# Reordering the helper work at the two ends of a Strassen-tiled ConvFFN: low parts, SiLU, the transfers of E and the last roundings

## The chip, the core and the metric

The kernel runs on one core of one Trainium2 chip. The metric is the device time of one execution in microseconds (us). A core has a matrix engine (TensorE, PE in the rows, its weight loads PEld), VectorE (DVE), ScalarE (ACT), GpSimd (POOL) and SyncE (SP, which here only issues DMAs). Each engine runs its own instructions in program order, and waits where an operand or a buffer isn't ready.

## The reference

A trunk of two residual layers on x of 1024 rows and 1024 columns, all float32. Layer 0 has a gated DeltaNet and a ConvFFN; then K and V are projected once; layer 1 has a chunked attention and a ConvFFN; a final RMSNorm ends it. The change touches the ConvFFN alone, which both layers have:

```python
def conv_ffn(xn, w_up, conv_w, conv_b, w_down):
    h = causal_dwconv(xn @ w_up, conv_w) + conv_b          # w_up 1024 x 5632, 3 taps
    gate, val = h[..., :FFN_DIM], h[..., FFN_DIM:]          # FFN_DIM = 2816
    return (jax.nn.silu(gate) * val) @ w_down

for layer in range(DEPTH):
    ...
    h = h + conv_ffn(rmsnorm(h, f_norm[layer]), f_w_up[layer], f_conv[layer], f_conv_b[layer], f_w_down[layer])
return rmsnorm(h, final_norm)
```

## The kernel before

**Numbers.** A float32 operand is cut into a high part (`uh`, `xh`: the value rounded to fp32r, a CAST on ScalarE) and a low part (`ul`, `xl`: value less high part, a TENSOR_TENSOR on VectorE or GpSimd). Each product is three matmuls: high by high (L1391), low data by high weight (L1392), high data by low weight (L1393).

**Tiles.** The up-projection has 22 channel tiles j of 128 gate and 128 value channels. Tiles 1 to 21 are each computed by seven products n = 1 to 7 in the manner of Strassen. `left_sum(j, n)` forms the weight sum of product n in place on VectorE (`r21`, `r11`, `r12` are the raw weight blocks, `r` in the rows), `operand(j, n)` rounds it on ScalarE (`uh`) and takes the low part (`ul`). The data sums `h<-h,h` with their roundings (`x7`, `xt2`, `xt1`, `xt4`, high and low) are made once at the start of the FFN. `after(j, n)` reads the accumulator banks: a copy `keep` on ScalarE for n = 1, `keep` and `keep7` on VectorE for n = 6, `vpre` and `gpre` for the rest. Product 2 adds onto the bank of product 1, and 4 onto that of 7, so each has to wait for the copy of that bank (`keep`, `keep7`).

**After a tile** come the three convolution taps of the value (`val`, v0 to v2) and of the gate (`gate`, g0 to g2): the first tap on ScalarE (ACTIVATE, L1483), the other two on VectorE (L1486). Then `silu` on ScalarE (L1489; with a table load where the table in the engine is another), `gated` (value times gate, VectorE), and `hidden` for the last three tiles (`hidh` on ScalarE, `hidl` on VectorE).

**The down-projection** runs in nine groups `("d", g, n)`, mixed into the same sequence; its weights are `a`, its roundings `dh`, `dl` and, for the channels, `eh`, `el`. Results go through `stage` tiles to DRAM by DMAs that add (`send`, issued by GpSimd). The product E is held apart in `d_e`: in the last group `load_e(u)` reads it back and `send_e(u, n)` adds it to three totals (n = 6, 7, 4) by three DMAs of 512 KB on GpSimd. The last weights of the down-projection, `fr`, are loaded by `load_last` and rounded by `cut_last(q)`: `fh` on ScalarE, `fl` on VectorE for even q and on GpSimd for odd q.

**What sets the order.** TensorE's work is a list of steps of 12 matmuls each: 0 to 7 are plain, 8 to 22 are the products of tiles 1 and 2 and the first of tile 3, 23 to 217 products of the tiles 3 to 21 with the down-projection's steps between them; the last up-projection steps are 211 (21,1), 212 (21,7), 213 (21,6), 214 (21,5), 215 (21,2), 216 (21,4) and 217 (21,3). Everything on the other engines is a job, placed by `at(i, f, rank)` in front of step i; jobs of one step are issued in the order of rank, and an engine keeps that order. `operand(j, n)` is placed two steps ahead of its product with rank 1. For the steps 8 to 16 (`i < early`) its low part is a job of its own on VectorE; later it is GpSimd's. `sums`, `highs` and `lows` of the data have ranks 1 to 2. The ring of up-projection weight parts has three buffers, those of `d` and `e` two. Weight loads of the up-projection are issued by SyncE (L1437).

```python
if i < early:
    low = []
    at(i - 2, lambda j=j, n=n, low=low: low.append(operand(j, n, False)), 1)
    at(i - 2, lambda low=low: low[0](), 2.5)
...
at(i + 2 + k // 2, lambda u=u, n=n: send_e(u, n), 0.6)
at(last_at[q], lambda q=q: cut_last(q), 1.5)
```

`fin_at` is the index of the last down-projection step of the last group, `pos[j, s]` the step at which tile j's part s starts, `nx(j, s)` that of tile j + 1, `end` the start of the last part.

Of the kernel before, what the change touches and what calls it, by code (L numbers as in the profile page):

```python
# [22 lines left out]
FP = 22  # L23
# [5 lines left out]
def trunk_kernel(  # L29
# [1323 lines left out]
    def ffn(layer, h, hp, xs, tail, d_r, last):  # L1353
# [19 lines left out]
        def at(i, f, rank=1):  # L1373

            jobs.setdefault(max(i, 0), []).append((rank, f))

        def cut_high(src, ring, copy=nc.scalar.copy):
            hi, lo = [(wd if ring == "e" else wf).tile([P, HALF], F32R, name=ring + x, tag=ring + x, bufs=RINGS[ring]) for x in "hl"]
            copy(hi, src)  # L1379
            return hi, lo  # L1380

        def cut_low(src, hi, lo, eng):
            tt(eng, lo, src, hi.bitcast(F32), sub)
# [58 lines left out]
        def left_sum(j, n):  # L1442
            a = lambda q: raw[j, q]
            if (j, n) in summed:
                return
            summed.add((j, n))
            if n == 7:
                tt(nc.vector, a(21), a(11), a(21), sub)
            elif n == 6:
                tt(nc.vector, a(21), a(22), a(21), sub)  # L1450
            elif n == 5:
                tt(nc.vector, a(11), a(21), a(11), add)
            elif n == 3:
                tt(nc.vector, a(12), a(12), a(21), sub)

        def operand(j, n, lo=True):

            a = lambda q: raw[j, q]
            left_sum(j, n)
            src = a({1: 11, 2: 12, 7: 21, 6: 21, 5: 11, 4: 22, 3: 12}[n])  # L1460
            ops[j, n] = cut_high(src, "u")
            if lo:
                cut_low(src, *ops[j, n], nc.gpsimd)
            return lambda: cut_low(src, *ops[j, n], nc.vector)
# [51 lines left out]
        def after(j, n):  # L1516
            p_ = bank[j, {2: 1, 4: 7, 3: 5}.get(n, n)]
            if n == 1:
                keep[j] = tp.tile([P, HALF], F32, name="keep", tag="keep", bufs=2)
                nc.scalar.copy(keep[j], p_)  # L1520
            elif n == 6:
                tt(nc.vector, keep[j], p_, keep[j], add)
                keep[j, 7] = tp.tile([P, HALF], F32, name="keep7", tag="keep7")
                tt(nc.vector, keep[j, 7], bank[j, 7], keep[j], add)
            elif n == 5:
                tt(nc.vector, new_pre(j, 1)[:, HALF:SEQ], p_, keep[j, 7], add)
            elif n == 2:
                nc.scalar.copy(new_pre(j, 0)[:, 0:HALF], p_)
            elif n == 4:
                tt(nc.vector, new_pre(j, 1)[:, 0:HALF], p_, keep[j], add)  # L1530
            elif n == 3:
                tt(nc.vector, new_pre(j, 0)[:, HALF:SEQ], p_, keep[j], add)
# [44 lines left out]
        end, fin_at = pos[FP - 1, 7], pos["d", NG - 1, 4]  # L1577
        early = pos["p", 1, 3]
        for i, (j, n) in due.items():
            if i < early:  # L1580
                low = []
                at(i - 2, lambda j=j, n=n, low=low: low.append(operand(j, n, False)), 1)
                at(i - 2, lambda low=low: low[0](), 2.5)
            else:
                at(i - 2, lambda j=j, n=n: operand(j, n), 1)
                if j > 3 and n in (6, 4):
                    at(i - 2, lambda j=j, n=n: left_sum(j, n - 1), 1.05)
            if n != 2 or j > 2:
                at(i + 1, lambda j=j, n=n: after(j, n), 0)

        def nx(j, s):
            return pos[j + 1, s] if j + 1 < FP else end + s
# [23 lines left out]
        for j in range(3, FP - 1):  # L1616
# [2 lines left out]

        v0, v1, v2, g0, g1, g2 = [(v, i) for v in (1, 0) for i in range(3)]  # L1620
        when = {
            0: [(11, (g0,), 0), (12, (v0,), 0), (13, (v1,), 2), (13, (v2,), 2.7), (15, (g1, g2, silu), 2), (17, (gated,), 2)],
            1: [(18, (v0, v1), 2), (19, (v2, g0), 2), (20, (g1,), 2), (21, (g2, silu), 2), (22, (gated,), 2)],
            2: [(24, (v0, v1), 2), (25, (v2, g0), 2), (26, (g1,), 2), (27, (g2, silu), 2), (28, (gated,), 2)],
        }
        for j in range(3, FP - 1):
            when[j] = [(pos[j, 7], (v0, v1), 2), (nx(j, 1), (v2, g0), 2), (nx(j, 2), (g1,), 2)]
            when[j] += [(nx(j, 3), (g2,), 2), (nx(j, 4), (silu,), 1.6), (nx(j, 5), (gated,), 2)]
            if j >= 2 * NG:
                when[j].append(({18: fin_at + 5, 19: fin_at + 7}.get(j, nx(j, 6)), (hidden,), 1.9))  # L1630
        for j, w_ in when.items():
            for i, fs, r in w_:
                at(i, lambda j=j, fs=fs: [taps(j, *f) if isinstance(f, tuple) else f(j) for f in fs], r)
# [82 lines left out]
        def total(n, u):  # L1716
            if n == 1:
                return d_e[u]
            c, s = where[n]
            return d_c[c, s, u]  # L1720
# [8 lines left out]
        def load_e(u):  # L1729
            stage["e", u] = hp.tile([P, SEQ], F32, name="stage", tag=f"h{layer + 1}_{(3, 4)[u]}")  # L1730
            nc.sync.dma_start(out=stage["e", u], in_=d_e[u])

        def send_e(u, n):
            nc.gpsimd.dma_start(out=total(n, u), in_=stage["e", u], accum_op=add)
# [21 lines left out]
        for u, i in ((0, pos["d", NG - 1, 5]), (1, fin_at + 2)):  # L1756
            at(i, lambda u=u: load_e(u), 3)
            for k, n in enumerate((6, 7, 4)):
                at(i + 2 + k // 2, lambda u=u, n=n: send_e(u, n), 0.6)


        k0 = 2 * NG
# [3 lines left out]
        last_at = [pos[FP - 1, s] for s in (3, 4, 5, 6)] + [end + 1] * 4  # L1766
        if layer == 1:
            last_at = [pos[FP - 1, 2]] + last_at[:-1]
# [16 lines left out]
        def cut_last(q):  # L1785
            k, s = slots[q]
            hi, lo = [actp.tile([P, HALF], F32R, name=f"f{x}{q}", tag=f"x{x}{k}_{s}") for x in "hl"]
            nc.scalar.copy(hi, fw[q])
            cut_low(fw[q], hi, lo, nc.gpsimd if q % 2 else nc.vector)
            fw[q] = hi, lo  # L1790

        for q in range(8):
            s = (1, 1, 2, 3, 4, 4, 5, 6)[q]
            at(fin_at + 1 if q < 2 else pos[FP - 1, s], lambda q=q: load_last(q), 1)
            at(last_at[q], lambda q=q: cut_last(q), 1.5)

        if layer == 0:

# [140 lines left out]
    d_h = [dram.tile([P, SEQ], F32, name=f"d_h{k}") for k in range(KT)]  # L1939
    xb = ([[None, None] for _ in range(KT)], [[None, None] for _ in range(KT)])  # L1940
    ctx_f, tail0 = ffn(0, h, hp, normed, tails[0], d_r0, xb)
    ctx_o = ctx.enter_context(ExitStack())
    wp = ctx_o.enter_context(tc.tile_pool(name="wp1", bufs=2, **SB))
# [288 lines left out]
    def norm_out(t, ht, fin):  # L2232
# [26 lines left out]
        return go()  # L2259

    ctx_f, _ = ffn(1, h, hp, normed, tails[0], d_r1, norm_out)
    ctx_f.close()
    ctx_h.close()
# [56 lines left out]
```

## Time and profile before

| | |
|---|---|
| median of 3 runs | 2615.96 us (2615.45 to 2617.17) |
| profiled execution | 2616.91 us, of which span 2615.1 us |
| granted clock of TensorE, mean | 0.994 |
| TensorE busy | 2517.5 us, 96% of the span |
| VectorE busy | 1862.1 us, 71% |
| ScalarE busy | 1413.1 us, 54% |
| GpSimd busy | 1485.5 us, 57% |
| up-projection and first down-projection steps of FFN0, FFN1 | 678 to 1298 us, 1932 to 2557 us |

A step of 12 matmuls takes 2.72 us where nothing is waited for. In the rows, an idle time in brackets stands in front of the instruction and names the instruction that ended it, as the profile infers it. "pu" is an accumulator bank of the up-projection, "r" a raw weight block, "x4" a group of four instructions on end.

### The profile page before, as it was taken

How to read it: one execution, taken by the hardware profiler on the slowest of the kernel's cores; microseconds unless marked ns; L12 is line 12 of the kernel's file. 1: busy time of each engine (PE TensorE's matmuls, PEld its weight loads, DVE VectorE, ACT ScalarE, POOL GpSimd, SP SyncE). 2: the span in 40 equal slices, each digit the busy share in tenths (PEclk: the TensorE clock that was granted, in tenths of full speed). 3: DMA queues.
4: the chain of work that ended last, by engine and by line, in shares of the span. 5: the costliest groups of instructions: out<-in, count | busy, mean ns of one | idle time of the engine just before them, and what ended most of it. 6: DMA issues, size and time to landing. Idle time of an engine off the chain costs nothing.

```text
span 2615.1 us, 39396 instructions
## 1 busy us (share of the span) xinstructions
PE 2517.5 (96%) x13933; PEld 2071.1 (79%) x13933; DVE 1862.1 (71%) x3102; ACT 1413.1 (54%) x2714; POOL 1485.5 (57%) x1472
## 2 busy tenths in 40 slices
PE   7999899999999999999999999998989999999998
PEld 5878788888777888888778888887867788888877
DVE  5765865554688888888775666665478788888875
ACT  5444455464455555655455555555345655555643
POOL 3655543345447777777645444443343777777771
PEclk9999999999999999999999999999999999999999
DMA  4534435555337677768831111114232567677795
GB/s 127 138 99 123 123 106 155 159 162 161 93 85 152 144 155 154 145 141 163 200 112 51 44 58 44 48 42 139 75 123 68 142 137 151 143 157 154 152 197 174
DMA packets 317590, 326.72 MB, mean 125 GB/s; under 512 B 32976, under 2 KB 240592, under 8 KB 317392
## 3 DMA queue, kind: packets, MB, share of 16 engines
q1 hardware_dynamic: 285936, 219.07, 28.5%
q0 software_dynamic: 26560, 96.48, 20.7%
q10 hardware_dynamic: 4896, 8.65, 0.9%
q8 instruction: 110, 1.80, 0.3%
q14 instruction: 88, 0.72, 0.1%
HBM read 180.94 MB, written 143.20 MB: 124 GB/s over the span
## 4 chain that ended last, share of the span: by engine, by line
PE 53%; POOL 5%; DVE 5%; issue 3%; ACT 2%; DMA 2%; DVEq 0%; POOLq 0%; ACTq 0%; SPq 0%
PE pu L1393 8%; PE pu L1391 8%; PE pu L1392 8%; PE pd L1392 4%; PE pd L1393 4%; PE pd L1391 4%; PE acc L120 3%; PE acc L121 3%; PE acc L122 3%; POOL ul L1358 2%; PE ptp L2070 2%; PE poT L2100 1%; PE poT L2099 1%; PE acco L120 1%; PE acco L121 1%
## 5 line engine op out<-in xcount | busy, mean ns | idle before, releaser
L1358 POOL TENSOR_TENSOR ul<-r,uh 128x512 fp32r<-128x512 f32 x282 | 445.7, 1600 | 297.6 <-ACT uh L1379 276.2
L120 PE MATMUL acc<-xh,whi 128*128 128x512 f32 x896 | 374.1, 418 | 0.3 <-ACT xh L1097 0.2
L121 PE MATMUL acc<-xl,whi 128*128 128x512 f32 x896 | 353.0, 394 | 1.8 <-POOL xl L379 0.9
L122 PE MATMUL acc<-xh,wlo 128*128 128x512 f32 x896 | 352.0, 393 | 0.5 <-POOL wlo L105 0.5
L105 POOL TENSOR_TENSOR wlo<-wraw,whi 128x256 fp32r<-128x256 f32 (+1 forms) x293 | 235.9, 834 | 197.7 <-ACT whi L103 157.3
L1379 ACT CAST uh<-r 128x512 fp32r<-128x512 f32 x296 | 181.9, 623 | 223.9 <-DVE r L1358 170.1
L1393 PE MATMUL pu<-xh,ul 128*128 128x512 f32 x552 | 216.6, 392 | 5.6 <-POOL ul L1358 5.5
L1391 PE MATMUL pu<-xh,uh 128*128 128x512 f32 x552 | 216.6, 392 | 3.0 <-ACT uh L1379 1.6
L1392 PE MATMUL pu<-xl,uh 128*128 128x512 f32 x552 | 215.8, 391 | 1.0 <-POOL xl L379 1.0
L1712 ACT COPY stage<-pd 128x1024 f32<-128x1024 f32 x180 | 174.9, 1013 | 50.0 <-PE pd L1393 49.4
L122 PEld LDWEIGHTS acc<-xh,wlo 128*128 128x128 f32 x896 | 168.4, 188 | 37.9 <-POOL wlo L105 0.9
L121 PEld LDWEIGHTS acc<-xl,whi 128*128 128x128 f32 x896 | 169.6, 189 | 26.6 <-POOL xl L379 3.1
L120 PEld LDWEIGHTS acc<-xh,whi 128*128 128x128 f32 x896 | 169.3, 189 | 22.9 <-ACT xh L1097 1.2
L1486 DVE SCALAR_TENSOR_TENSOR val<-vpre,colt,val 128x1023 f32<-128x1023 f32 (+2 forms) x92 | 153.4, 1668 | 38.6 <-ACT val L1483 38.4
L1358 POOL TENSOR_TENSOR dl<-a,dh 128x512 fp32r<-128x512 f32 x90 | 155.0, 1722 | 38.4 <-ACT dh L1379 38.4
L1486 DVE SCALAR_TENSOR_TENSOR gate<-gpre,colt,gate 128x1023 f32<-128x1023 f32 (+2 forms) x92 | 175.4, 1906 | 0.8
L2050 POOL TENSOR_SCALAR sS<-sS,st 128x640 f32<-128x640 f32 (+4 forms) x128 | 88.3, 693 | 140.5 <-DVE st L2049 122.7
L1358 DVE TENSOR_TENSOR r<-r,r 128x512 f32<-128x512 f32 x168 | 131.5, 782 | 31.0 <-POOL ul L1358 29.6
L2048 ACT ACTIVATE sS<-sS,st 128x640 f32<-128x640 f32 (+4 forms) x128 | 89.2, 697 | 82.3 <-DVE st L2047 81.3
L1393 PEld LDWEIGHTS pu<-xh,ul 128*128 128x128 f32 x552 | 104.0, 188 | 31.3 <-POOL ul L1358 9.8
L1391 PEld LDWEIGHTS pu<-xh,uh 128*128 128x128 f32 x552 | 104.1, 189 | 25.7 <-ACT uh L1379 2.4
L1392 PEld LDWEIGHTS pu<-xl,uh 128*128 128x128 f32 x552 | 104.2, 189 | 23.6 <-POOL xl L379 2.1
(389 smaller groups left out, 7107.9 us busy)
## 6 DMA issues: line engine op xcount, KB each, us to landing
r<-in_f_w_up_dram SPq DMA_DIRECT2D x168, 256.0 KB, 4.4
d_r<-stage POOLq DMA_DIRECT2D x78, 512.0 KB, 8.1
d_c<-stage POOLq DMA_DIRECT2D x70, 512.0 KB, 8.1
a<-in_f_w_down_dram SPq DMA_DIRECT2D x72, 256.0 KB, 2.8
wraw<-in_a_w_in_dram SPq DMA_DIRECT2D x32, 512.0 KB, 4.6
d_e<-stage POOLq DMA_DIRECT2D x32, 512.0 KB, 9.2
wraw<-in_a_w_out_dram SPq DMA_DIRECT2D x16, 512.0 KB, 4.2
d_r<-h ACTq DMA_DIRECT2D x32, 256.0 KB, 4.0
```

Of the source, the lines that this page charges most:

```text
L105: nc.gpsimd.tensor_tensor(lo[:, c], raw[:, c], hi[:, c].bitcast(F32), op=ALU.subtract)
L120: mm(ps, hi[:, kw, wcol : wcol + P], rh[k][s], start=st, stop=False)
L121: mm(ps, hi[:, kw, wcol : wcol + P], rl[k][s], start=False, stop=False)
L122: mm(ps, lo[:, kw, wcol : wcol + P], rh[k][s], start=False, stop=sp)
L1358: tt = lambda eng, o, a, b, op: eng.tensor_tensor(o, a, b, op=op)
L1379: copy(hi, src)
L1391: mm(ps, w[0][:, cw], x[0], start=first, stop=False, skip_group_check=True)
L1392: mm(ps, w[0][:, cw], x[1], start=False, stop=False, skip_group_check=True)
L1393: mm(ps, w[1][:, cw], x[0], start=False, stop=last, skip_group_check=True)
L1486: nc.vector.scalar_tensor_tensor(t_[:, a:c1], p_[:, a - step : c1 - step], w[:, 2 - step : 3 - step], t_[:, a:c1], op0=ALU.mult, op1=ALU.add)
L1712: nc.scalar.copy(t_, ps)
L2048: nc.scalar.activation(S, S, AF.Exp, bias=st[:, 1:2], accum_out=st[:, 2:3])
```

## The change

Six edits of where helper jobs stand; no instruction is added or taken away, and TensorE's order is as it was.

```diff
@@ operands
-                at(i - 2, lambda low=low: low[0](), 2.5)
+                at(i - 2, lambda low=low: low[0](), 1.9)
             else:
                 at(i - 2, lambda j=j, n=n: operand(j, n), 1)
+                if j == FP - 1 and n == 1:
+                    at(i - 2, lambda j=j: left_sum(j, 7), 1.05)
@@ taps
-            0: [(11, (g0,), 0), (12, (v0,), 0), (13, (v1,), 2), (13, (v2,), 2.7), (15, (g1, g2, silu), 2), (17, (gated,), 2)],
-            1: [(18, (v0, v1), 2), (19, (v2, g0), 2), (20, (g1,), 2), (21, (g2, silu), 2), (22, (gated,), 2)],
-            2: [(24, (v0, v1), 2), (25, (v2, g0), 2), (26, (g1,), 2), (27, (g2, silu), 2), (28, (gated,), 2)],
+            0: [(11, (g0,), 0), (12, (v0,), 0), (13, (v1,), 2), (13, (v2,), 2.7), (15, (g1, g2), 2), (16, (silu,), 1.6), (17, (gated,), 2)],
+            1: [(18, (v0, v1), 2), (19, (v2, g0), 2), (20, (g1,), 2), (21, (g2,), 2), (22, (silu,), 1.6), (23, (gated,), 1.1)],
+            2: [(24, (v0, v1), 2), (25, (v2, g0), 2), (26, (g1,), 2), (27, (g2,), 2), (28, (silu,), 1.6), (29, (gated,), 2)],
...
-                when[j].append(({18: fin_at + 5, 19: fin_at + 7}.get(j, nx(j, 6)), (hidden,), 1.9))
+                when[j].append(({18: fin_at + 5, 19: fin_at + 7}.get(j, nx(j, 6)), (hidden,), 1.9 if j == 18 else 0.95))
@@ E
-                at(i + 2 + k // 2, lambda u=u, n=n: send_e(u, n), 0.6)
+                at(i + 2 + k, lambda u=u, n=n: send_e(u, n), 0.6 if (u, n) == (0, 4) else 2.9)
@@ last weights
-            at(last_at[q], lambda q=q: cut_last(q), 1.5)
+            at(last_at[q], lambda q=q: cut_last(q), 0.9 if q < (4 if layer == 0 else 2) else 1.5)
```

1. The low part of an early operand goes from rank 2.5, behind the data's sums and low parts of its step, to 1.9, in front of them.
2. The weight sum of product (21,7) is made two steps ahead of (21,1).
3. SiLU of tiles 0, 1 and 2 is placed one step later, and `gated` of the tiles 1 and 2 too.
4. `hidden(19)` and, by the same token, `hidden(20)` come at rank 0.95 of their step.
5. The three transfers of E are one step apart, behind the step's other jobs (rank 2.9).
6. The first roundings of the last weights (four in layer 0, two in layer 1) come in front of the step's operand.

VectorE, FFN0, around the operand of step 14 (1,5). The names: `r11` is its weight sum, `ul_7900` its low part, `ul_7873` that of step 13, `xt4l` the low parts of the data of product 4. Before:

```order
L1358 TENSOR_TENSOR ul_7873<-r21_7538,uh_7872 128x512
L1358 TENSOR_TENSOR r11_7548<-r21_7538,r11_7548 128x512
L1358 TENSOR_TENSOR xt4l0_7573<-h1_4_6467,xt4h0_7572 128x512
L1358 TENSOR_TENSOR xt4l1_7575<-h1_5_6468,xt4h1_7574 128x512
L1358 TENSOR_TENSOR xt4l2_7577<-h1_6_6469,xt4h2_7576 128x512
L1358 TENSOR_TENSOR xt4l3_7579<-h1_7_6470,xt4h3_7578 128x512
L1358 TENSOR_TENSOR ul_7900<-r11_7548,uh_7899 128x512
```

VectorE, the same place, after:

```order
L1358 TENSOR_TENSOR r11_7548<-r21_7538,r11_7548 128x512
L1358 TENSOR_TENSOR ul_7900<-r11_7548,uh_7899 128x512
L1358 TENSOR_TENSOR xt4l0_7573<-h1_4_6467,xt4h0_7572 128x512
L1358 TENSOR_TENSOR xt4l1_7575<-h1_5_6468,xt4h1_7574 128x512
L1358 TENSOR_TENSOR xt4l2_7577<-h1_6_6469,xt4h2_7576 128x512
L1358 TENSOR_TENSOR xt4l3_7579<-h1_7_6470,xt4h3_7578 128x512
L1358 TENSOR_TENSOR r21_7760<-r11_7594,r21_7760 128x512
```

The low part `ul_7900` went from behind the four `xt4l` to the place right behind its own sum `r11_7548`; `ul_7873` stands further ahead in the same way.

ScalarE, FFN0, from the `keep` copy of product (21,1) on. `uh` from `r11` is for step 214, from `r12` for step 215, from `r22` for step 216. Before:

```order
L1520 COPY keep_12615<-pu1_12602 128x512
L1379 CAST uh_12617<-r11_12458 128x512
L1379 CAST uh_12637<-r12_12573 128x512
L1788 CAST fh0_12643<-fr_12500 128x512
L1503 CAST hidh_12647<-val_12363 128x1024
L1379 CAST uh_12668<-r22_12506 128x512
L1788 CAST fh1_12677<-fr_12502 128x512
L1489 ACTIVATE gate_12600<-gate_12600 128x1024
```

ScalarE, the same place, after:

```order
L1520 COPY keep_12614<-pu1_12601 128x512
L1379 CAST uh_12616<-r11_12458 128x512
L1790 CAST fh0_12637<-fr_12500 128x512
L1503 CAST hidh_12641<-val_12363 128x1024
L1379 CAST uh_12645<-r12_12572 128x512
L1790 CAST fh1_12668<-fr_12502 128x512
L1379 CAST uh_12672<-r22_12506 128x512
L1489 ACTIVATE gate_12598<-gate_12598 128x1024
```

`fh0` and `hidh` went in front of the rounding of `r12`, and `fh1` in front of that of `r22`.

GpSimd, FFN0, the second set of E's transfers, before:

```order
L1358 TENSOR_TENSOR ul_12547<-r11_12458,uh_12546 128x512
L1734 DMA d_r0011_92<-stage_12530 128x1024
L1734 DMA d_r0111_96<-stage_12530 128x1024
L1358 TENSOR_TENSOR ul_12567<-r21_12436,uh_12566 128x512
L1734 DMA d_r0101_94<-stage_12530 128x1024
L1358 TENSOR_TENSOR ul_12591<-r21_12436,uh_12590 128x512
```

GpSimd, the same place, after:

```order
L1358 TENSOR_TENSOR ul_12547<-r11_12458,uh_12546 128x512
L1358 TENSOR_TENSOR ul_12565<-r21_12436,uh_12564 128x512
L1736 DMA d_r0011_92<-stage_12530 128x1024
L1358 TENSOR_TENSOR ul_12589<-r21_12436,uh_12588 128x512
L1736 DMA d_r0111_96<-stage_12530 128x1024
L1358 TENSOR_TENSOR ul_12617<-r11_12458,uh_12616 128x512
L1736 DMA d_r0101_94<-stage_12530 128x1024
```

The two transfers that stood next to each other are one low part later and one apart, the third one two low parts later.

## Rows read from the trace of the kernel before

**Rows 1.** Stretches; busy us (count) of each engine, TensorE clock, DMA share, GB/s:

```profile
1298.28:1330.92 32.64, 32.64 (x145) 27.03 (x144) 25.37 (x34) 20.05 (x43) 7.88 (x4) 1.00 0.60 204
711.95:740.72 28.77, 25.83 (x109) 19.77 (x108) 27.13 (x36) 14.64 (x20) 8.54 (x5) 1.00 0.24 74
751.60:774.48 22.88, 20.52 (x85) 15.38 (x84) 19.58 (x19) 15.92 (x23) 12.03 (x9) 1.00 0.44 103
1235.50:1245.38 9.88, 8.81 (x37) 6.60 (x36) 9.06 (x7) 4.93 (x9) 6.70 (x7) 1.00 0.79 144
1277.80:1298.28 20.48, 16.65 (x62) 12.12 (x61) 16.57 (x13) 9.19 (x14) 11.34 (x7) 0.92 0.71 180
1968.05:1999.99 31.94, 27.82 (x109) 21.01 (x109) 28.83 (x38) 16.02 (x23) 8.57 (x5) 0.95 0.22 66
2010.87:2033.22 22.35, 20.41 (x85) 15.38 (x84) 19.22 (x19) 15.37 (x22) 10.17 (x7) 1.00 0.30 106
2492.08:2501.67 9.59, 8.77 (x37) 6.52 (x36) 9.07 (x7) 4.70 (x8) 6.41 (x6) 1.00 0.79 149
2534.34:2556.54 22.20, 17.96 (x61) 13.18 (x60) 18.79 (x15) 10.20 (x17) 12.32 (x8) 0.85 0.92 250
```

**Rows 2.** Timeline of TensorE: start, us, instruction, idle before:

```profile
721.41 0.50 PE L1393 MATMUL pu<-xt1h,ul 128*128 128x512 f32 x1 [0.61 <-DVE ul L1358]
...
735.61 0.50 PE L1393 MATMUL pu<-xt2h,ul 128*128 128x512 f32 x1 [1.73 <-POOL ul L1358]
...
1291.27 0.76 PE L1391 MATMUL pu<-xt4h,uh 128*128 128x512 f32 x1 [2.77 <-DVE keep L1358]
```

**Rows 3.** Timeline of VectorE, start of FFN0:

```profile
701.27 2.49 DVE L1358 TENSOR_TENSOR x7l<-h,x7h 128x512 fp32r<-128x512 f32 x4
...
720.67 0.69 DVE L1358 TENSOR_TENSOR ul<-r,uh 128x512 fp32r<-128x512 f32 x1
...
736.20 1.68 DVE L1486 SCALAR_TENSOR_TENSOR val<-vpre,colt,val 128x1023 f32<-128x1023 f32 x1 [1.17 <-ACT val L1483]
```

**Rows 4.** Timeline of ScalarE, start of FFN0:

```profile
701.79 0.63 ACT L1379 CAST uh<-r 128x512 fp32r<-128x512 f32 x1
...
715.36 2.43 ACT L1421 CAST xt4h<-h 128x512 fp32r<-128x512 f32 x4
717.69 1.24 ACT L1483 ACTIVATE val<-vpre,colt 128x1024 f32<-128x1024 f32 x1
718.84 0.60 ACT L1379 CAST uh<-r 128x512 fp32r<-128x512 f32 x1
...
728.82 1.28 ACT L1489 ACT_TABLE_LOAD   x1
731.52 1.06 ACT L1489 ACTIVATE gate<-gate 128x1024 f32<-128x1024 f32 x1 [1.41 <-DVE gate L1486]
```

**Rows 5.** Timeline of ScalarE, step 22 of FFN0:

```profile
750.69 1.06 ACT L1489 ACTIVATE gate<-gate 128x1024 f32<-128x1024 f32 x1 [3.20 <-DVE gate L1486]
```

**Rows 6.** Timeline of VectorE, step 198 of FFN0:

```profile
1235.90 3.91 DVE L1358 TENSOR_TENSOR r<-r,r 128x512 f32<-128x512 f32 x1 [2.12 <-POOL ul L1358]
```

**Rows 7.** Timelines of ScalarE and VectorE, ends of FFN0 and FFN1:

```profile
1283.91 0.62 ACT L1379 CAST uh<-r 128x512 fp32r<-128x512 f32 x1 [4.30 <-PE pu L1393]
...
1280.74 2.30 DVE L1486 SCALAR_TENSOR_TENSOR gate<-gpre,colt,gate 128x1023 f32<-128x1023 f32 x1
1285.08 1.35 DVE L1358 TENSOR_TENSOR fl<-fr,fh 128x512 fp32r<-128x512 f32 x1 [2.04 <-ACT fh L1788]
...
2545.40 0.62 ACT L1788 CAST fh<-fr 128x512 fp32r<-128x512 f32 x1 [1.42 <-DMA fr<-in_f_w_down_dram]
```

**Rows 8.** DMA issues of 1269 to 1284; KB each, us to landing:

```profile
r<-in_f_w_up_dram SPq DMA_DIRECT2D x1, 256.0 KB, 15.1
```

**Rows 9.** Timeline of ScalarE, final norm:

```profile
2580.84 1.28 ACT L2252 ACT_TABLE_LOAD   x1
2582.13 0.29 ACT L2252 ACTIVATE ss<-ss,epst 128x1 f32<-128x1 f32 x1
```

## The prediction

> **What bounds the kernel now.** I read the table of stretches first [rows 1]. Its first row is an undisturbed stretch near the end of FFN0: TensorE is busy for all of its 32.64 us, in 144 matmuls, so a matmul takes 0.2267 us and a step of 12 takes 2.72. The next four rows are the stretches of FFN0 that the change touches, the last four the same ones in FFN1. A stretch's loss is its width less its matmuls (the count of weight loads; 61 and 60 in the two ends) times 0.2267:
>
> - start, steps 11 to 19, 108 matmuls, 24.48 us: 28.77 − 24.48 = 4.29 lost; FFN1 31.94 − 24.48 = 7.46.
> - steps 22 to 29, 84, 19.04: 3.84 and 3.31.
> - steps 198 to 200, 36, 8.16: 1.72 and 1.43.
> - end, steps 213 to 217: 20.48 − 13.83 = 6.65 and 22.20 − 13.60 = 8.60.
>
> Together 37.3 us, the most the change could reach. TensorE bounds; it loses time only where an operand's part or an accumulator's bank comes late. The idle rows of TensorE [rows 2] name what comes late: VectorE's `ul` at 721.41 (0.61), GpSimd's `ul` at 735.61 (1.73), VectorE's `keep` at 1291.27 (2.77).
>
> **Part 1, low parts in front of the four sums (steps 8 to 16): a loss.** Nothing is added; the order on VectorE changes. There VectorE is the engine without slack: from `x7l` at 701.27 on each of its rows follows its predecessor, up to the first gap, 1.17 us ahead of 736.20 [rows 3]; TensorE's wait at 721.41 is the end of the `ul` of 720.67 plus 0.05. Today four sums or low parts (2.41 us, pitch 0.60) stand between an operand's sum `r` and its `ul`, and cover the round trip VectorE to ScalarE and back: 0.11 hop, cast 0.62, 0.03 hop (ends to starts in the timelines of rows 3 and 4). Without them VectorE waits. By hand, with the new order and the durations of rows 3 and 4:
>
> - `ul` of step 9 wants to start at 701.27 (where `x7l` stands). Its `uh` is cast at 701.79 today, behind ScalarE's `xt2h` and a copy, which now start 0.6 later: 701.79 + 0.6 + 0.62 + hops is 703.11. Wait 1.84.
> - step 12: round trip behind a `keep` copy, 1.2; step 13: 0.75.
> - step 14: its `uh` (718.84 today) stands on ScalarE behind `xt4h` x4 (2.43) and a first tap (1.24) [rows 4]: 1.83. Step 15: 0.76.
>
> The sum is 6.4 us on an engine that has no slack. A moved `ul` itself comes 2.41 earlier relative to its neighbours, so step 14 loses 6.4 − 0.76 − 2.41 = 3.2 us, while all that is behind (the taps, `keep7`) loses the whole. At step 20 I get 747.2 for 740.7, 6.5 lost; the same chain from FFN1's rows gives 4.75 (its start has 3.17 more loss already, which absorbs some). FFN1's granted clock in this stretch is 0.95 in the mean, in FFN0 1.00: after long waits there were microseconds at the lower level of 1.2 GHz. For that 0.4 each. **Part 1: 12.0 lost**, bounds 8 (FFN1 absorbs more, the copy-bound waits shorter) and 15 (clock as in FFN1's row in both: 0.05 × 28.8 = 1.4 each, and no absorption).
>
> **Part 2, SiLU a step later.** For tile 0 the table load (1.28) and the SiLU [rows 4] now stand behind one more `uh`. Today ScalarE's queue stands 1.41 for VectorE's `gate` at 731.52, with the next `uh` behind it, which leads to the 1.73 at 735.61. In the new chain VectorE is 6 late anyway, so this gain is inside part 1's 747.2 and isn't counted again. Tiles 1 and 2 (steps 22 to 30) are independent: SiLU waits 3.20 for the taps at 750.69 [rows 5] and the `keep` copy and `uh` stand behind it. Replaying ScalarE's queue with those two in front recovers 1.6 and 1.9 of 3.84, and 1.04 and 1.88 of 3.31: **6.4 gained** (5 to 6.6; the ceiling is 7.15). `gated` of tile 1 moves behind one more `r`; it is read two steps later, so I price that at nothing.
>
> **Part 3, E's transfers one step apart, in the last down-projection group.** GpSimd's three sends come behind `ul`s and `dl`. Today VectorE's `r` waits 2.12 for a `ul` that stands behind sends and then runs 3.91 [rows 6], where the `ul` of 720.67 [rows 3], of the same size, takes 0.69. With the `ul` in front, steps 198 to 200 recover 1.65 of 1.72 and 1.39 of 1.43: **3.0 gained** (2 to 3.15). The sends come 1 to 2 steps later; their readers are tens of microseconds away.
>
> **Part 4, end (steps 213 to 217).** Four edits meet here. `uh` of step 215 starts at 1283.91, put down to TensorE after 4.30 of idle [rows 7]; really its source `r12` landed just then, for a transfer of that stretch took 15.1 us [rows 8] while E's sends filled the same DMA engines. Behind this `uh` on ScalarE stand `fh0` and `hidh`; VectorE's `fl` waits 2.04 for `fh` at 1285.08 [rows 7] and `keep7`, which TensorE needs, comes after `fl`, `hidl` and the taps at 1291.27. In the new order `fh0` and `hidh` go first: `fl` follows the taps of 1280.74 at about 1283, `hidl` at 1284.3, the next taps at 1285.4, `keep7` at 1286 to 1287.5 instead of 1291.2. I take r12's landing at 1280 to 1282, for the sends leave gaps between them. The last step of the stretch (217) then ends at 1292.4 instead of 1298.28 [rows 1]: 5.85 gained (4.5 to 6.6, the ceiling being the loss of 6.65). In FFN1 `keep7` no longer ends the chain; next is `fr`'s landing, which gives `fh` at 2545.40 [rows 7], with the SiLU and the last `uh` behind it: 5.6 gained (4 to 6.5). **11.45 gained.** If r12 lands no earlier, only the order on ScalarE is left, and the two ends gain 3.4. left_sum(21,7) early and `hidden`(19) at 0.95 serve the same chain; one 0.60 and one 2.1 on VectorE, in front of work that waits for TensorE anyway: nothing.
>
> **Sum.** Gains 6.4 + 3.0 + 11.45 = 20.85, loss 12.0, net 8.85. The profiled execution: span 2615.1 − 8.85 = 2606.25, plus 1.8 outside the span 2608.05. It is 0.95 above the median of the runs, so against the median 2607.1.
>
> **The rivals.**
>
> - *Start costs nothing*: the round trips find slack that my chain lacks, and the low parts merely come sooner. For it: the wait at 721.41 is for exactly such a `ul`. Against: VectorE has no idle between 701.27 and 735. 2607 − 12 = 2595.
> - *The transfers are no faster*: r12 lands as late, because the rings stay full with the other streams. Gain 6.4 + 3.0 + 3.4 − 12.0 = 0.8: 2615.
> - *Start loses more*: taps, `keep7` and the table load in one serial chain, 17 instead of 12: 2612.
> - *Slower*: the new waits at the starts keep TensorE at 1.2 GHz for the steps 14 to 20 of both FFNs. Seven steps are 19 us at full clock; if two thirds of them run at half, that is 12.7 more per FFN, and the loss is 12 + 25.4 = 37.4 against gains of 20.85: 16.55 slower, 2632.5; with it in one FFN only, 3.85 slower, 2619.8. It decides as soon as the starts lose more than 20.85. For it: FFN1's start has 0.95 of clock today; against: FFN0's stays at 1.00 with a wait of 1.73 in it.
> - *Nothing moves*: gains and loss are taken back by the next wait: 2616.
> - *The switch of tables drains the engine*. Rows: the load at 2580.84 takes 1.28 and the next activation starts at 2582.13 [rows 9], so no more is seen than the load; the 1.41 behind the load of 728.82 is put down to VectorE. Were those 1.41 a part of the switch, they would stand in part 1's serial chain, twice 1.41: 2610. The Trainium skill, "ScalarE: Activation LUTs", section "What ACT_TABLE_LOAD costs", speaks for this rival: it gives 1283 ns for the load and 1380 ns of drain for every switch. The load agrees with the trace; the drain does not show at 2582.13.
>
> **How the numbers follow.** The runs of this kernel lie within 0.07% of each other, so 0.2%, 5.2 us, is what can be told from no change: faster is below 2610.8, slower above 2621.2. Chances: forecast (2603 to 2611) 0.48, start for nothing 0.12, transfers no faster 0.11, start loses more 0.09, slower 0.12, nothing moves 0.04, drain 0.04. Faster: 0.44 of the forecast, 0.12 and 0.02 of the drain: 0.58. Slower: 0.10 of the 0.12 (its lower figure is inside 0.2%). Same: the rest, 0.32. The extremes of the bounds are 2615.96 − (13.1 + 6.6 + 3.15 − 8) = 2601 and 2615.96 − (8.5 + 5 + 2 − 15) = 2615.5; the range goes down to 2598, half-way into the case without a loss at the start, and up to 2616, and leaves out about 0.18.
>
> **What would show it.** Right: idle rows of VectorE put down to ScalarE's `uh` between 701 and 725, step 20 some 6 us late in FFN0 and 4 to 5 in FFN1; no 3.20 wait of the SiLU in front of `keep`; VectorE's `r` near step 199 back at 0.7; `r12` of step 215 in about 12 us, TensorE's wait of 2.77 gone, the ends some 5 us shorter. Wrong: no new idle on VectorE at the start, or `r12` still 15 us, or a granted clock of one half through the starts.

## The result and the profile after

The changed kernel takes 2628.87 us in the median of 4 runs (2627.81 to 2629.65), the kernel before 2616.57 in runs beside it: ratio 1.0042, 95% interval 1.003 to 1.0053. It is 12 us slower; the forecast was 9 us faster, in a range up to 2616. The profiled execution took 2627.81 with a span of 2626.0, against 2615.1.

TensorE's matmuls can be set side by side one by one, since its order is the same. The table gives, for the starts of a few steps, how much later or earlier they come than in the profile of before, as differences from one mark to the next (us); a stretch runs from the start of its first step to the start of the step behind its last. The last three columns are kernels of the next section.

| stretch | changed kernel | low parts alone | first transfers alone | ends alone |
|---|---|---|---|---|
| all ahead of step 3 of FFN0 | +0.51 | +0.91 | +2.25 | +2.49 |
| FFN0, steps 3 to 21 | **+7.33** | +6.55 | +0.01 | 0.00 |
| FFN0, 22 to 37 | −0.48 | +0.05 | +0.02 | +0.03 |
| FFN0, 198 to 206 | **+3.54** | −0.06 | +1.84 | +0.01 |
| FFN0, 213 to 216 | −2.67 | −1.10 | −0.25 | −2.62 |
| FFN0's step 217 to FFN1's step 2 | +0.57 | −0.17 | +0.45 | +1.11 |
| FFN1, 3 to 21 | **+5.68** | +4.89 | −1.65 | −1.65 |
| FFN1, 22 to 37 | −1.02 | +0.53 | +0.54 | +0.55 |
| FFN1, 198 to 206 | **+4.07** | 0.00 | +5.58 | +0.01 |
| FFN1, 213 to 216 | −6.85 | −0.40 | −0.28 | −6.87 |
| rest | +0.2 | +0.1 | +0.4 | +0.4 |
| span | +10.9 | +11.3 | +8.9 | −6.6 |

Two things have to be read off such a table first. The first row is the stage ahead of the FFN, which is the same code in all kernels, and ends between 1.8 us earlier and 10.6 us later than in the profile of before. And in every kernel that leaves FFN1's start alone, this start comes out 1.65 shorter and the steps 22 to 37 0.53 longer, so the profile of before has some 1.1 us there by chance, and likewise, by most of these kernels, about 1.1 at the end of FFN0. The 1.65 lie in a stretch in which that profile's granted clock is at the lower level, as in a row of [rows 1]:

```profile
1994.10:1997.50 3.40, 3.40 (x10) 2.62 (x9) 1.71 (x2) 0.69 (x2) 2.53 (x2) 0.50 0.02 6
```

It follows a wait of TensorE of 1.73; behind the same wait in FFN0 [rows 2] the clock stays at 1.00, and in the kernels that leave this start alone it does so in FFN1 too.

The stretches of the changed kernel, in the form of [rows 1]: the start of FFN0 (from the end of step 10 to step 20), its steps 24 to 30 (those of the row at 751.60, which the prediction calls 22 to 29), 31 and 32, 198 to 200, 201 to 205, and 213 to the end of 217; then the start of FFN1 and its steps 201 to 205 and 213 to 217.

```profile
712.62:748.44 35.82, 28.51 (x109) 20.64 (x109) 28.52 (x39) 16.60 (x24) 8.21 (x5) 0.95 0.19 59
759.46:778.92 19.46, 19.46 (x85) 15.49 (x83) 17.85 (x18) 11.84 (x18) 10.51 (x8) 1.00 0.47 113
778.76:788.98 10.22, 7.35 (x25) 5.76 (x25) 4.08 (x6) 9.02 (x12) 6.54 (x5) 0.83 0.27 71
1243.05:1251.21 8.16, 8.16 (x37) 6.76 (x36) 6.29 (x4) 3.97 (x6) 6.87 (x7) 1.00 0.65 98
1251.21:1270.07 18.86, 15.78 (x61) 12.29 (x60) 14.15 (x15) 7.61 (x11) 11.52 (x10) 0.91 0.84 181
1289.11:1306.68 17.57, 15.14 (x60) 12.05 (x59) 16.37 (x13) 7.59 (x12) 11.57 (x7) 0.90 0.73 174
1977.00:2014.54 37.54, 28.92 (x109) 20.61 (x109) 30.24 (x41) 18.29 (x26) 8.23 (x5) 0.95 0.19 57
...
2513.87:2533.00 19.13, 15.78 (x62) 12.26 (x60) 14.16 (x15) 7.60 (x11) 11.52 (x10) 0.91 0.83 180
2552.04:2567.22 15.18, 14.09 (x61) 11.06 (x60) 14.03 (x12) 8.67 (x14) 11.51 (x7) 1.00 1.05 295
```

With 0.2267 us for a matmul, steps 198 to 200 lose nothing now (36 in 8.16 us): that gain is as forecast. Right behind it the steps 201 to 205, 60 matmuls or 13.60 us, take 18.86 and 19.13, where they took 13.60 in FFN0 before (1245.39 to 1258.99). Steps 24 to 30 lose 0.4 instead of 3.84, and steps 31 and 32, 5.44 us at full clock, take 10.22. The new waits of TensorE, FFN0 (start, us, instruction, idle before and what ended it):

```profile
781.79 0.50 PE L1391 MATMUL pd<-eh,dh 128*128 128x512 f32 x1 [2.87 <-ACT stage L1714]
...
1261.81 0.51 PE L1391 MATMUL pu<-x7h,uh 128*128 128x512 f32 x1 [2.27 <-ACT uh L1379]
...
1299.87 0.47 PE L1391 MATMUL pu<-xt4h,uh 128*128 128x512 f32 x1 [2.43 <-DVE keep L1358]
```

The first stands at step 31, the second at step 204, where TensorE hadn't waited at all; the third is [rows 2]'s wait of 2.77 for `keep7`, still there. The granted clock falls behind each: 0.83, 0.91 and 0.90 in the three stretches, 1.00 in the two without a wait.

### The profile page after: what moved, and what is told of

The parts are those of the page before. It is cut to its first block, busy times and chain, and to the rows that moved or that the text cites. A ratio compares the mean times of both kernels' runs of the same rounds, so it can differ in the third digit from the quotient of the medians.

```text
span 2626.0 us, 39396 instructions
## 1 busy us (share of the span) xinstructions
PE 2520.0 (96%) x13933; PEld 2077.2 (79%) x13933; DVE 1866.9 (71%) x3102; ACT 1413.3 (54%) x2714; POOL 1482.1 (56%) x1472
## 4 chain that ended last, share of the span: by engine, by line
PE 54%; DVE 5%; POOL 4%; issue 3%; ACT 2%; DMA 2%; DVEq 0%; POOLq 0%; ACTq 0%; SPq 0%
PE pu L1393 8%; PE pu L1391 8%; PE pu L1392 8%; PE pd L1391 4%; PE pd L1392 4%; PE pd L1393 4%; PE acc L120 3%; PE acc L121 3%; PE acc L122 3%; PE ptp L2072 2%; POOL ul L1358 1%; PE poT L2102 1%; PE poT L2101 1%; PE acco L121 1%; PE acco L122 1%
```

## The experiments

Each kernel is the kernel before with the edit shown, except `undo_two`. "Slower" and "faster" are against runs of the kernel before on the same chip. Every kernel here ran once, but `undo_two` ran ten times and `best` eight; the kernel before ran once beside `low_only`, `silu_only`, `e0_only` and `ends_only` and 12 or 13 times beside the others, between 2613.66 and 2620.40, a wider spread than the three runs that the prediction had. So the total of a single run is good to some 3 us, and what a part does is read from the stretches.

**low_only**: the low parts alone.

```diff
-                at(i - 2, lambda low=low: low[0](), 2.5)
+                at(i - 2, lambda low=low: low[0](), 1.9)
```

> The kernel before with the early low parts in front of the sums, and nothing else. Theory (VectorE waits for ScalarE's rounding, no slack): step 20 comes some 7 us later in FFN0 and 5 to 6 us later in FFN1, as in the changed kernel; the whole is 12 to 14 us slower, about 2629. Rival (most of the loss at the start is tile 0's SiLU with its table load, which the changed kernel has in the serial chain): 8 us slower or less, about 2624.

Measured 2628.12 against 2618.2: 9.9 slower. Step 16 comes 6.4 us later in FFN0 (from +0.9 ahead of the start to +7.3). VectorE's timeline at this start:

```profile
703.96 0.69 DVE L1358 TENSOR_TENSOR ul<-r,uh 128x512 fp32r<-128x512 f32 x1 [1.69 <-ACT uh L1379]
...
714.77 0.69 DVE L1358 TENSOR_TENSOR ul<-r,uh 128x512 fp32r<-128x512 f32 x1 [1.09 <-ACT uh L1379]
...
719.24 0.69 DVE L1358 TENSOR_TENSOR ul<-r,uh 128x512 fp32r<-128x512 f32 x1 [0.77 <-ACT uh L1379]
...
724.67 0.69 DVE L1358 TENSOR_TENSOR ul<-r,uh 128x512 fp32r<-128x512 f32 x1 [1.73 <-ACT uh L1379]
...
729.19 0.69 DVE L1358 TENSOR_TENSOR ul<-r,uh 128x512 fp32r<-128x512 f32 x1 [0.82 <-ACT uh L1379]
```

Five waits that were not there, 6.1 us in all, each for ScalarE's rounding; the prediction had 1.84, 1.2, 0.75, 1.83 and 0.76. The rival, that tile 0's SiLU makes most of this loss, falls: it adds 0.8 (7.33 less 6.55). FFN1 loses as much: 4.89 above a profile that has 1.65 there by chance.

**low_14**: one low part of the nine.

```diff
-                at(i - 2, lambda low=low: low[0](), 2.5)
+                at(i - 2, lambda low=low: low[0](), 1.9 if (j, n) == (1, 5) else 2.5)
```

> The kernel before with one early low part alone in front of the sums, that of step 14, (1,5), the one for which TensorE waits 0.61 at step 14. Theory (on VectorE, which has no slack here, the wait for ScalarE's rounding costs more than the order gains): VectorE stands about 1.2 us in front of this ul, TensorE's 0.61 at step 14 is gone, but keep7 and what follows come about 1.2 later and step 16 or 20 loses 0.5 to 1 us in each FFN on balance. Rival (the change went wrong only because all nine low parts were moved): 0.4 to 0.6 us gained in each FFN at step 14 and kept to step 20.

VectorE's timeline at the moved low part:

```profile
721.53 0.69 DVE L1358 TENSOR_TENSOR ul<-r,uh 128x512 fp32r<-128x512 f32 x1 [1.14 <-ACT uh L1379]
```

VectorE stands 1.14, and TensorE's wait at step 14 is gone; but all that is behind it on VectorE is later by it. At step 15 TensorE now waits for the rounding of a sum `r` that VectorE makes behind this low part:

```profile
726.07 0.50 PE L1391 MATMUL pu<-x7h,uh 128*128 128x512 f32 x1 [0.92 <-ACT uh L1379]
```

By step 18 both starts have lost 1.24, a little more than the 0.5 to 1 expected. So even the one low part for which TensorE waited is better left behind the sums. In all, the starts come out longer by 2.84 in FFN0 and 1.18 in FFN1 (2.84 with the 1.65); in FFN0 1.58 of it come at step 19, and the granted clock of the stretch (712 to 745) is 0.95 instead of 1.00. The clock is at 0.50 from 739.0 to 742.4. Whether this belongs to the edit stays open: `ends_keep7`, which leaves this start alone, has the same from 740.3 on and 1.24 at the same step, and the 1.65 by chance of before lie in FFN1's steps 18 and 19. The total was 2621.75 against 2616.98.

**silu_only**: the SiLU edit alone (three lines of the table of taps, as in the diff of the change).

```diff
-            2: [..., (27, (g2, silu), 2), (28, (gated,), 2)],
+            2: [..., (27, (g2,), 2), (28, (silu,), 1.6), (29, (gated,), 2)],
```

> The kernel before with SiLU and the gating product of the tiles 0 to 2 a step later, and nothing else. Theory (the later SiLU of tile 2 stands between dh and the stage copies, and TensorE waits at step 31 for the stage copy): steps 25 and 26 gain 1.5, step 30 0.8, a wait of 2 to 3 us at step 31 takes it back; 0 to 3 us faster in all. Rival (the wait at step 31 comes from VectorE being late through the low parts): no wait at step 31, and the 6.4 us of the prediction.

2616.5 against 2618.2. Up to the start of step 26 it gains 1.6, up to that of step 30 another 0.8, and step 31 waits 2.89 us, as in the changed kernel (2.87): steps 22 to 37 come out at −0.44 and −0.69 instead of −3.5 and −2.9. Tile 0's SiLU costs 0.78 at the start. So the wait at 31 belongs to this edit, not to the low parts. What makes it is seen in the changed kernel, on VectorE's timeline first:

```profile
772.57 4.20 DVE L1486 SCALAR_TENSOR_TENSOR gate<-gpre,colt,gate 128x1023 f32<-128x1023 f32 x2
```

and then on ScalarE's, up to the copies that TensorE waits for:

```profile
778.78 0.62 ACT L1379 CAST dh<-a 128x512 fp32r<-128x512 f32 x1 [4.65 <-DVE a L1358]
779.30 1.05 ACT L1489 ACTIVATE gate<-gate 128x1024 f32<-128x1024 f32 x1
780.26 0.56 ACT L1528 COPY gpre<-pu 128x512 f32<-128x512 f32 x1
780.73 1.93 ACT L1714 COPY stage<-pd 128x1024 f32<-128x1024 f32 x2
```

The `stage` copies, which free the accumulator for step 31, stand on ScalarE behind `dh`, which waits for VectorE's `a`; `a` comes behind the taps. SiLU used to go ahead of `dh`, while ScalarE waited anyway; now it stands between `dh` and the copies. And the pair of taps takes 4.20 instead of 2.59 (766.38 to 768.97 before), since GpSimd now makes its `ul` at the same time (773.99, 1.69 us, where it started at 770.71 before, after the taps).

**silu_t2**: SiLU of tiles 1 and 2 a step later, tile 2's in front of `dh`; tile 0 as before.

```diff
-            2: [..., (27, (g2, silu), 2), (28, (gated,), 2)],
+            2: [..., (27, (g2,), 2), (28, (silu,), 1.05), (29, (gated,), 2)],
```

> The kernel before with SiLU of the tiles 1 and 2 a step later, tile 0 as before, and tile 2's SiLU right behind the operand's rounding, in front of dh and the stage copies. Theory (two things make the stage copy late at step 31: SiLU between dh and the copies, 1.0, and VectorE's second gate tap, which takes 2.9 us instead of 1.3 while GpSimd makes a low part): the wait at step 31 falls from 2.9 to about 1.9 us in FFN0; in all 1 to 4 us faster than the kernel before. Rival (the SiLU's place is all): the wait goes.

TensorE at step 31:

```profile
778.97 0.50 PE L1391 MATMUL pd<-eh,dh 128*128 128x512 f32 x1 [1.89 <-ACT stage L1712]
```

The wait falls from 2.89 to 1.89, as expected of SiLU's 1.05. The remaining 1.9 is put down to the taps, which take 4.21 here too, 1.6 more than before; no run has the later SiLU with short taps. Steps 22 to 37: −1.44 and −1.54; the total was 2616.03 against 2616.46.

**e0_only**: the first set of E's transfers alone.

```diff
-                at(i + 2 + k // 2, lambda u=u, n=n: send_e(u, n), 0.6)
+                at(i + 2 + (k if u == 0 else k // 2), lambda u=u, n=n: send_e(u, n), 2.9 if u == 0 and n != 4 else 0.6)
```

> The kernel before with the first set of E's transfers (u = 0) one step apart, and nothing else. Theory (the stage buffer that these transfers read is the room of tile 19's val, whose first tap on ScalarE has to wait until the last transfer has landed): 1.5 gained at step 200 in each FFN, 5 to 5.5 lost at steps 204 and 205; 7 to 8 us slower. Rival (the stall at 204 needs the other edits, for the transfers land before the tap when the rest of the queue is as before): 3 us faster.

2625.68 against 2618.2: 7.5 slower, with the gains of steps 198 to 200 (1.73 and 1.43) and the stall at 204 both there. ScalarE in front of step 204, in the timeline of the kernel before:

```profile
1245.34 1.26 ACT L1483 ACTIVATE val<-vpre,colt 128x1024 f32<-128x1024 f32 x1
```

The same instruction here, and the next one on ScalarE:

```profile
1251.54 1.25 ACT L1483 ACTIVATE val<-vpre,colt 128x1024 f32<-128x1024 f32 x1 [2.55 <-DMA d_r<-stage]
1255.46 0.62 ACT L1379 CAST uh<-r 128x512 fp32r<-128x512 f32 x1 [2.68 <-DVE r L1358]
```

`val` is the first tap of tile 19. Its room is that of tile 3, 7, 11 and 15, and this same room holds E between `load_e(0)` and the last of the three transfers (both have the tag `h…_3`, lines 1480 and 1730 of before). In the kernel before the last transfer landed at 1245.07, 0.27 us ahead of the tap: nothing to be seen as a wait, and no slack either. Here GpSimd, with the second and third transfer now behind `el` (the third keeps its rank 0.6, one step later), issues them at 1242.85 and 1243.44, the last lands at 1251.51, and the tap starts at 1251.54. Behind the tap are VectorE's taps and `r`, then `uh` of step 204, then TensorE:

```profile
1256.13 0.50 PE L1391 MATMUL pu<-x7h,uh 128*128 128x512 f32 x1 [1.69 <-ACT uh L1379]
```

In FFN1 the margin of before was 1.54 (landing 2500.33, tap 2501.87); here the tap stands 4.03 for the landing, and TensorE 3.16 for `uh`. The landing isn't all that makes the tap late: ScalarE had also stood 3.15 for VectorE's `a`, which took 3.52 beside GpSimd's later `ul`s, where it took 1.17 before. But ScalarE was through with that at 1248.99, and the 2.55 and 4.03 that it then stood for the landing alone are more than TensorE's waits of 1.69 and 3.16. No kernel was run in which E has a room of its own.

**e0_one_ul**: the three transfers next to each other, none behind `el`: the first two one `ul` later than before, the third behind the same `ul` as before.

```diff
-                at(i + 2 + k // 2, lambda u=u, n=n: send_e(u, n), 0.6)
+                at(i + 2 + (k // 2 if u else 0), lambda u=u, n=n: send_e(u, n), 0.6 if u else 2.9)
```

> The kernel before with the first set of E's three transfers all behind one more low part (that of step 199) and next to each other, none of them behind el. Theory (only the landing of the last one counts, since tile 19's first tap needs the room): it lands within 1.5 us of where it landed before, steps 198 to 200 gain 1.5 in each FFN as in the kernel with the transfers one step apart, and step 204 loses 0 to 2 instead of 3.5 and 6.6: between 3 faster and 1 slower in all. Rival (the transfers being later at all takes DMA time from the weight loads, and the uh of step 204 is late for that): step 204 loses as much as before, 6 us slower or more.

2613.23, beside 2616.46 as the median of before. The tap of tile 19 on ScalarE:

```profile
1246.73 1.24 ACT L1483 ACTIVATE val<-vpre,colt 128x1024 f32<-128x1024 f32 x1 [1.11 <-DMA d_r<-stage]
```

The first two transfers are issued 2 us later than before, but the last one lands at 1246.70, the tap waits 1.11, and TensorE does not wait at step 204: steps 198 to 206 come out at −0.11 and −0.40. Not the lateness of the transfers as such but the landing of the last one decides. (`a` took 1.03 here, so this run alone doesn't part the landing from the longer `a`; the waits of `e0_only` do.) The gain of steps 198 to 200 is 0.47 instead of 1.73, for a reason that has its place in the last section.

**ends_only**: what the change does at the end.

```diff
+                if j == FP - 1 and n == 1:
+                    at(i - 2, lambda j=j: left_sum(j, 7), 1.05)
...
-(hidden,), 1.9))
+(hidden,), 1.9 if j == 18 else 0.95))
...
+ send_e: one step apart and at 2.9 for u = 1 only
...
-            at(last_at[q], lambda q=q: cut_last(q), 1.5)
+            at(last_at[q], lambda q=q: cut_last(q), 0.9 if q < (4 if layer == 0 else 2) else 1.5)
```

> The kernel before with the edits at the end alone: sum of (21,7) early, hidden 19, the second set of E's transfers (u = 1) one step apart, the last roundings in front. Theory (what the changed kernel shows between the steps 205 and 217): 2.5 gained in FFN0, where keep7 stays the last to come, VectorE being busy in front of it, and 6.5 in FFN1: 9 us faster, about 2607.5. Rival (the prediction's): 5.9 and 5.6, 11.5 faster; r12 lands in under 8 us in both.

2610.34 against 2618.2: 7.9 faster. FFN1's end gains 6.87 (about 6.5 without the chance share), FFN0's only 2.62, of which 1.1 by chance, and the wait for `keep7` is 2.45. In the changed kernel `r12` of step 215, issued at 1279.37, landed 6.7 us later, instead of 15.1 [rows 8]; the DMA issues of 1279 to 1287:

```profile
r<-in_f_w_up_dram SPq DMA_DIRECT2D x1, 256.0 KB, 6.7
```

So the transfer is no longer what is late. VectorE in the changed kernel, from the taps that [rows 7] has at 1280.74 to `keep7`:

```profile
1289.93 2.31 DVE L1486 SCALAR_TENSOR_TENSOR gate<-gpre,colt,gate 128x1023 f32<-128x1023 f32 x1
1292.17 1.78 DVE L1358 TENSOR_TENSOR fl<-fr,fh 128x512 fp32r<-128x512 f32 x1
1293.87 2.31 DVE L1358 TENSOR_TENSOR hidl<-val,hidh 128x1024 fp32r<-128x1024 f32 x1
1296.10 2.30 DVE L1486 SCALAR_TENSOR_TENSOR gate<-gpre,colt,gate 128x1022 f32<-128x1022 f32 x1
1298.32 1.40 DVE L1358 TENSOR_TENSOR keep<-pu,keep 128x512 f32<-128x512 f32 x2
```

There is no idle in it: 8.39 us from the taps to `keep`, 8.98 before. VectorE is the bound here, with each of its instructions longer than elsewhere (a tap 1.27 and `hidl` 1.21 in the kernel before, `fl` 0.68 at 1300.84 here); GpSimd makes low parts beside it from 1289.52 to 1297.31.

**ends_keep7**: the ends, with `fl0` and `hidden(19)` of FFN0 behind `keep7`.

```diff
-... 19: fin_at + 7}.get(j, nx(j, 6)), (hidden,), ...
+... 19: fin_at + 7 + (layer == 0)}.get(j, nx(j, 6)), (hidden,), ...
-            at(last_at[q], lambda q=q: cut_last(q), ...
+            at(last_at[q] + (layer == 0 and q == 0), lambda q=q: cut_last(q), ...
```

> The edits at the end, and in FFN0 fl0 and hidden 19 one step later still, so that on VectorE keep7 of tile 21 comes in front of them (in layer 1 nothing differs from the kernel with the ends alone). Theory (in FFN0 keep7 is the last to come because VectorE has fl0, 1.7 us, and hidl, 2.2 us, in front of it): the 2.45 us wait at step 216 goes, 2 to 3 us faster than with the ends alone. Rival (keep7 waits for TensorE's products or a transfer, not for VectorE's queue): the wait stays, no difference.

The wait at step 216 is gone, and the end of FFN0 comes out at −6.64 instead of −2.62. But the total is 2610.99, no better than the ends alone: between step 217 and FFN1 3.54 go again. TensorE in FFN0's last projection and the norm behind it, where the kernel before has only the second wait, with 0.78:

```profile
1331.73 0.50 PE L1391 MATMUL pf<-hidh,fh 128*128 128x512 f32 x1 [1.19 <-DVE h L1358]
1337.91 1.05 PE L370 MATMUL pss<-ones,nacc 128*128 128x2 f32 x8 [1.81 <-DVE nacc L367]
```

The theory holds for the wait and misses the total. What ends this wait chain is VectorE's `h` and `nacc`, for which ScalarE squares `h` in turn with scaling the K/V weights (L96). About 2.4 of the 3.5 is seen there (1.35 and 1.03 in the starts behind the two waits); the other 1.2 goes in step 217 itself, where TensorE waits 0.89 for GpSimd's `ul`. Nothing was tried against either.

**undo_two**: the changed kernel less the low parts and the first transfers.

> The changed kernel with two of its parts taken back: the early low parts stand behind the sums again, and the first set of E's transfers (u = 0) where it stood; the SiLU edit, the second set of transfers and the end are as changed. Theory (the four single parts add up): 9 us from the ends, 0 to 1.5 from SiLU: 9 to 10.5 faster than the kernel before, ratio about 0.9963. Rival (the parts hinder each other, the SiLU being worth its predicted 6.4 once nothing else is late): 15 to 18 faster, ratio 0.9935.

Ratio 0.9979, 0.9970 to 0.9989: 5.5 us faster than the kernel before (6.9 between the medians, 2609.59 and 2616.46), not 9 to 10.5. FFN0's end gains 3.93 there and 3.53 are lost up to FFN1, with waits of 0.80 and 1.80 at the two places just shown, and tile 0's and 2's SiLU keep FFN0's steps 3 to 37 at +1.2. That the two parts taken out are the whole of the slowdown stands: with them 1.0042, without them 0.9979.

**best**: `ends_keep7` and tile 1's SiLU alone.

> What the single runs leave of the change: the sum of (21,7) early, the second set of E's transfers (u = 1) one step apart, the last roundings in front with fl0 and hidden 19 of FFN0 behind keep7, and the later SiLU for tile 1 alone; low parts, tiles 0 and 2, and the first set of transfers as before. Theory (the stretches add up): FFN0's end 5.5 less 2.6 given back in its last projection, FFN1's end 6.3, tile 1's SiLU 1.6 and 1.0: 11 to 13 faster, ratio about 0.9955. Rival (the gain of FFN0's end is given back whole, in the projection and the norm behind it): 8 to 9 faster, ratio 0.9967.

Ratio 0.9973, 0.9962 to 0.9984: median 2610.84 (2607.11 to 2615.07) beside 2616.98. By the interval it is faster than the kernel before; the gain is below what was expected, nearer to the rival's 0.9967: the end of FFN0 gains 6.64 and 2.97 are given back. Counted by stretches from step 3 of FFN0 on, its profile is 13 us shorter than that of before (10 to 11 without the chance shares); in that profile the stage ahead had 10.6 us more. Why the median shows 6 and not 10 isn't settled.

## Why the prediction was wrong

**Part 1 held.** Five waits of VectorE for ScalarE's rounding, 6.4 forecast, 6.1 measured; steps 3 to 21 lose 6.55 and 4.89 for 12.0 forecast. One piece of it was wrong: "its start has 3.17 more loss already, which absorbs some". FFN1 absorbs nothing; half of the 3.17 more was chance, and it loses the same 6.5 as FFN0. That FFN1's figure came out all the same (5.15 forecast with 0.4 for the clock, 4.89 measured) is luck: the profile of before holds 1.65 there by chance.

**Part 3 failed**, and it is the largest piece of the miss, 10.6 of the 19.75 us between 8.85 faster and 10.9 slower: 3.0 gained was forecast, 7.6 lost was measured (3.54 and 4.07). The gain of steps 198 to 200 came as forecast, 1.73 and 1.43 for 1.65 and 1.39. The step that failed is the sentence "The sends come 1 to 2 steps later; their readers are tens of microseconds away". It asks who reads what the transfers write. It doesn't ask who next writes what they read. That was tile 19's first tap, 0.27 us behind the last landing in FFN0 and 1.54 in FFN1, and 5.3 and 5.5 us of stall and lowered clock at steps 204 and 205 went for it. The rows stood in the trace of before (the landing at 1245.07, the tap at 1245.34), with no idle time on them, so no view of waits could show them.

**Part 2's mechanism was half right**: 6.4 forecast, 1.5 measured. Tile 1 gave its 1.6 and 1.0. Tile 2 gave 0.8 of 1.9 and then met the `stage` copies of step 31. The failed step is "Replaying ScalarE's queue with those two in front recovers 1.6 and 1.9 of 3.84": the replay followed the `uh` up to step 30 and stopped there, while ScalarE's queue behind the later SiLU holds the copies that step 31 needs. It also kept VectorE's tap at its old length, although the `ul` that comes earlier on GpSimd falls into it.

**Part 4** was 11.45 forecast, 9.5 measured (2.67 and 6.85). In FFN1 it was better than forecast. In FFN0 `r12` came earlier than forecast and it gave less, for `keep7` was put at "1286 to 1287.5": that counted 5.3 to 6.8 us from the taps to `keep7`, with `fl` at 1.3 and `hidl` at 1.1, near the 1.35 and 1.21 that they took in the kernel before, at another place in GpSimd's queue. With the measured 1.7, 2.2 and twice 2.2 it is 8.4. So the 5.85 was mis-sized by the length of VectorE's instructions (2.67 measured, some 1.1 of it by chance), and `ends_keep7` shows the rest: had the 5.85 come, about half of it would have gone again in step 217, the projection and the norm behind.

**The sum**: 12 lost at the starts (13.0 measured with tile 0's SiLU), gains of 20.85 forecast, and of these 9.5 and 1.5 came, and 7.6 were lost where 3.0 was to be gained. 13.0 − 9.5 − 1.5 + 7.6 = 9.6, and 1.3 of the other stretches makes the 10.9 of the spans. The rival on the slower side had the wrong mechanism (TensorE at the lower clock through steps 14 to 20; the granted clock of the starts is 0.95). The rival of a switch of tables that drains the engine is answered by the changed kernel, on ScalarE's timeline:

```profile
739.88 1.28 ACT L1489 ACT_TABLE_LOAD   x1
741.17 1.06 ACT L1489 ACTIVATE gate<-gate 128x1024 f32<-128x1024 f32 x1
```

The SiLU starts 0.01 us behind the end of the load, in FFN1 as well (2007.25 and 2007.26), so the switch takes the 1.28 and no more; the 1.41 of before, and the 1.42 in `low_only`, were a wait for VectorE's `gate`. (The Trainium skill's page "ScalarE: Activation LUTs", section "What ACT_TABLE_LOAD costs", gives 1380 ns of drain for every switch; no such time shows behind these loads, and here the measurement decides.)

## What to carry to other kernels

Before a transfer, a copy or any reader is moved later, ask who writes its source buffer next, and compare the two times in the trace even if nothing waits there: a margin of 0.27 us leaves no idle time that a view of waits could show. In a queue that runs in order, replay what stands behind the moved instruction until the next thing that the bounding engine waits for, not until the wait that was to go. And take an instruction's time from rows in which the same neighbours run beside it.

## What the runs showed of the hardware

Beside GpSimd a two-input TENSOR_TENSOR on VectorE took 3.3 to 5.1 us instead of 0.68. VectorE's `val` in `e0_one_ul`:

```profile
1235.48 5.10 DVE L1358 TENSOR_TENSOR val<-val 128x512 f32<-128x512 f32 x1
```

GpSimd in the same stretch of the same kernel:

```profile
1234.78 2.69 POOL L1734 DMA_DIRECT2D d_r<-stage  x3
1236.47 2.32 POOL L1358 TENSOR_TENSOR ul<-r,uh 128x512 fp32r<-128x512 f32 x1
1237.72 2.30 POOL L1358 TENSOR_TENSOR dl<-ay,dh 128x512 fp32r<-128x512 f32 x1
```

VectorE's instruction ends at 1240.58, 0.56 after GpSimd's second one (1240.02). In the kernel before it is the same: the `r` of [rows 6] ends at 1239.81, GpSimd's `dl` (1237.01, 2.25) at 1239.26, 0.55 ahead. In `e0_only` 1240.61 and 1240.06. So the 3.91 of [rows 6] ends with the second of two GpSimd instructions on end, and whichever VectorE instruction falls beside them pays: that is why `e0_one_ul`, with `r` at 0.69 and `val` at 5.10, gains only 0.47 in steps 198 to 200. The Trainium skill, "SBUF — State Buffer", section "Who interferes with whom", says that a VectorE instruction with two inputs in SBUF contends with a GpSimd instruction that reads SBUF. The three pairs agree, and they show besides that the block can last through two GpSimd instructions.

Two on end are not enough for that, though. In the kernel before, VectorE:

```profile
832.11 1.78 DVE L1358 TENSOR_TENSOR val<-val 128x512 f32<-128x512 f32 x1
```

and GpSimd beside it:

```profile
831.63 1.71 POOL L1358 TENSOR_TENSOR ul<-r,uh 128x512 fp32r<-128x512 f32 x1 [0.16 <-ACT uh L1379]
833.29 1.75 POOL L1358 TENSOR_TENSOR dl<-ay,dh 128x512 fp32r<-128x512 f32 x1
```

This `val` ends at 833.89, 0.55 after the first of the two (833.34), and so do 96 more such instructions in the kernel before, none of them with a transfer's issue beside it. Four end behind the second, and beside each of these four GpSimd also issues a transfer (in [rows 6] the one of 1235.14). In `e0_one_ul` `val` even starts 0.99 ahead of GpSimd's first `ul` (1236.47), while such issues run. An issue alone is not it either: the `r` ahead of that `val` took 0.69 beside one. So the long block goes with two GpSimd instructions and an issue; what part the issue has was not tried.

Before the FFN, code that is the same in every kernel took between 0.8 us less and 5.3 us more than in the profile of before, part of it in jumps (about 1.5 us between 250 and 300 us in seven of the eleven other profiles), and up to 5.3 more in the first steps of FFN0. These jumps go with the granted clock: those seven, and no other, have it at 0.50 around 270 us, and `best` from 686.0 to 696.2. Stretches that two kernels share mostly agreed to about 0.1 us (FFN0's steps 198 to 206 within 0.12), but not all: FFN0's start has 1.61 more in `ends_keep7`, which leaves it alone, and FFN1's end 0.92 less in `silu_t2`. The totals of single runs were not as good.
